# Rotary scores from two half-height parts, and the second rotary product ahead of the first head group

## The chip, the cores and the metric

The kernel runs on one NeuronCore of a Trainium2 chip. The metric is the device time of one execution in microseconds (us), of which lower is better. Engines are named as in the profile: PE (TensorE, with PEld for its weight loads), DVE (VectorE), ACT (ScalarE), POOL (GpSimd), SP (SyncE, which issues the weight transfers).

## The reference

Two decoder layers on 256 tokens of width 2048, each an attention mixer followed by a gated feed-forward block. Layer 1, which the change touches, is multi-head latent attention with 16 heads. From the normed input `h` it computes `cq = rms_norm(h @ wq_a)` (512 wide), from that the queries, 192 wide for each head: 128 plain columns `q_nope` and 64 rotary columns `q_rope`. From `h @ wkv_a` (576 wide) come the 512 latent columns `ckv` and ONE rotary key of 64 columns that all heads share. The scores of a head are

```
s = (q_nope . k_nope + q_rope . k_rope) * 192 ** -0.5     # causal, then softmax, then p @ v
```

All of it is in float32; the reference's rotary part is normed by head, multiplied by a gain and rotated with the position.

## The kernel before

Every large product is taken in "fp32r", a float32 form that TensorE runs in one pass, on a high part (the value rounded) and a low part (what the rounding left): high by high, high by low, low by high. Each weight piece of 128 x 512 is split by `Stream.split` (L92): ACT casts the high part (L104), DVE subtracts it (L105). Small products inside attention are plain float32 (F32), which TensorE runs as two instructions each.

The order of all work is written by hand. `quanta` is a list of PE products, one for each weight piece; `add` appends one and returns its index. `at(q, f)` hangs side work behind quantum q. The loop at L1049 goes through the quanta: it first splits pieces up to four ahead of q (L1052), then issues the product of q, then q's side work. Each engine executes its own instructions in the order in which that loop issues them, so DVE, ACT and POOL each have one queue, in which weight splitting and side work alternate. The weight units (4 pieces, 1 MB) are loaded on SP's queue three units ahead of the split (L96, L71); `units` (L138 to L155) must list them in the order of the quanta.

Layer 1's attention stage is planned from L818. Its quanta, in order:

- `wq_a` (16 quanta, `feat_major`), which leaves `cqT`.
- `rotary_queries(0, 2)` (L985): 4 quanta of `mla_wqr`, the rotary queries of heads 0 to 7. Its side work (`Heads` with 8 heads a tile, 64 wide): evacuation at its last quantum, squares, `rstd` on POOL, scaling, rotation, and 28 and 29 quanta after its last one the transposes `turned` (L442) and the copy `turned_out` (L454) into `qrT`.
- `wkv_a` (2 x 16 quanta, 288 columns each). Call the last of them q. Behind q hang `kva_stats` (L839, with a POOL power at L852), at q+3 `kva_scale` (L854), at q+3 and q+4 `kva_turn` (L878: transposes of `ckv`, evacuated into `ckvT`), at q+7 `kva_rotate` (L864), at q+9 `kr_turn` (L891: transposes of the rotary key).
- four head groups g of 4 heads: 4 quanta each of queries (`cqT`), keys and values (`ckvT`), in the order q, k, v for g = 0 and k, q, v after that. Behind group 0 stands `rotary_queries(1, 2)` (L1015), the rotary queries of heads 8 to 15. `plan_heads` (L622) hangs the norm and the transposes of each product behind it, `Head.plan` (L556) the head's scores (L474), softmax, transposes of the probabilities (`turn`, `turned`) and values.

For the rotary scores a tile of `qrT` holds two heads: the even head's 64 rotary rows on partitions 0 to 63, the odd head's on 64 to 127. `kr_turn` writes two key tiles of 128 rows, one with the key on the upper 64 rows and zeros below, one the other way round (POOL writes the zeros at L898, DVE copies at L899). The rotary product of a head (L489) is therefore a float32 product over 128 rows, of which 64 are multiplied by zeros. Per head there are two query blocks: 128 key columns for the first and 256 for the second.

Of the kernel before, what the change touches and what calls it, by code (L numbers as in the profile page):

```python
# [115 lines left out]
def trunk(ctx: ExitStack, tc: tile.TileContext, a, out):  # L116
# [28 lines left out]
    units += units_of("mla_wq_a")  # L145
    units += grouped("mla_wqr", 1, 0)
    units += units_of("mla_wkv_a", KVN)
    for g in range(4):
        if g == 1:
            units += grouped("mla_wqr", 1, 1)  # L150
        for name in ("mla_wkn", "mla_wqn", "mla_wv") if g else ("mla_wqn", "mla_wkn", "mla_wv"):
            units += grouped(name, 1, g)
    units += units_of("mla_wo")
# [199 lines left out]
    class Heads:  # L353
# [21 lines left out]

        def squares(self, t):
            for i in range(self.n):
                junk = att_pool.tile([P, P], F32, name="junk", bufs=2)
# [38 lines left out]
        def rotate(self, t, stages=(0, 1)):  # L417
            if not self.rot:
                return
            n, rot = self.n, self.rot  # L420
            hf = rot // 2
            tb, C, Sn = self.tabs
            ct = tb[:, C + t * rot : C + (t + 1) * rot]
            st = tb[:, Sn + t * rot : Sn + (t + 1) * rot]
            x = self.x[:, t]
            def over(s):
                return s[:, None, :].to_broadcast([P, n, s.shape[1]])

            def part(name):
                r = att_pool.tile([P, 16 * 32], F32, name=name, bufs=2)  # L430
# [38 lines left out]
    class Head:  # L469
# [4 lines left out]
        def scores(self):  # L474
            sc = ps_sc.tile([P, 512], F32, name="sc")
            qT, kT, i = self.qT(), self.kT(), self.i
            self.sc = sc
            if self.parts:

                (q0, q1), (k0, k) = qT, kT  # L480
                mm(sc[:, :P], q0[:, i], k0[:, i], start=True, stop=True)
                three(sc[:, P : 3 * P], q1[:, 0, i], q1[:, 1, i], k[:, 0, i], k[:, 1, i], True, True)
                return
            for q0, n, c in ((0, P, 0), (P, S, P)):
                o = sc[:, c : c + n]
                mm(o, qT[:, i, q0 : q0 + P], kT[:, i, :n], start=True, stop=self.rope is None)  # L486
                if self.rope is not None:
                    qr, kr = self.rope()
                    mm(o, qr[:, q0 : q0 + P], kr[:, :n], start=False, stop=True)  # L489

        def biased(self):
            self.s = att_pool.tile([P, 3 * P], F32, name="s", bufs=3)
# [30 lines left out]

        def turned(self):
            if not self.parts:
                self.pT = att_pool.tile([P, 3 * P], F32, name="pT", bufs=2)
# [294 lines left out]
    def open_mla():  # L821
        nonlocal att_pool
        ffn["stack"].close()
        att_pool = att2.enter_context(tc.tile_pool(name="att2", bufs=2))
        env["ckv"] = att_pool.tile([P, NT, 2 * KVN], F32, name="ckv", bufs=1)
        env["ckvT"] = att_pool.tile([P, 4, 2 * S], F32R, name="ckvT", bufs=1)
        env["cqT"] = att_pool.tile([P, 4, 2 * S], F32R, name="cqT", bufs=1)
        env["oT"] = att_pool.tile([P, H, 2 * S], F32R, name="oT", bufs=1)
        env["qrT"] = att_pool.tile([P, 8, S], F32, name="qrT", bufs=1)


    def kva_evac(state, half):
# [6 lines left out]
    def kva_stats():  # L839
        ss = small.tile([P, NT, 2], F32, name="kvss")  # L840
        for t in range(NT):
            for k, (lo, hi) in enumerate(((0, 512), (512, 576))):
                junk = att_pool.tile([P, 512], F32, name="kvjunk", tag="ro1", bufs=2)
# [18 lines left out]
            )  # L862

    def kva_rotate():  # L864
        env["krr"] = att_pool.tile([P, NT, 2, 64], F32, name="krr", bufs=1)
        for t in range(NT):
            x = env["ckv"][:, t, 512:]
            ct = tab[:, T_LC + t * 64 : T_LC + (t + 1) * 64]
            st = tab[:, T_LS + t * 64 : T_LS + (t + 1) * 64]
            t1 = att_pool.tile([P, 64], F32, name="kro1", bufs=2)  # L870
            t2 = att_pool.tile([P, 64], F32, name="kro2", bufs=2)
# [19 lines left out]
    def kr_turn():  # L891
        tp = ps_tp.tile([P, 512], F32, name="tp")
        for t in range(NT):
            nc.tensor.transpose(
                tp[:, t * P : (t + 1) * P], env["krr"][:, t].rearrange("p i d -> p (i d)"), ident
            )
        for i in range(2):
            nc.gpsimd.memset(env["kr"][i], 0.0)  # L898
            nc.vector.tensor_copy(env["kr"][i][i * 64 : (i + 1) * 64, :], tp[i * 64 : (i + 1) * 64, :S])  # L899


    cq = {}
# [54 lines left out]

    at(q_start + 20, gained_tables)

    def rotary_queries(u, step):  # L960
        state = {}
        for kt in range(4):
            q = add(tok_major, state, lambda: env["cqT"], kt, 3)
# [29 lines left out]
    def open_room():  # L993
        t = keep.tile([P, KD * 2 * S + 64], F32, name="room", tag="h")
        env["room"] = t[:, : 32 * S].rearrange("p (k s) -> p k s", k=32)
        env["kr"] = [env["room"][:, 28 + i] for i in range(2)]

    at(q, open_room)
    at(q, kva_stats)
    at(q + 3, kva_scale)  # L1000
    at(q + 7, kva_rotate)
    for r in range(4):
        at(q + 3 + r // 2, kva_turn, r)
    at(q + 9, kr_turn)

    def mla_tiles(g):
        i = 4 * (g % 2)
# [3 lines left out]
        env["v", g] = env["room"][:, 16 + i : 20 + i].rearrange("p (t c) s -> p t (c s)", t=NT)  # L1011

    for g in range(4):
        if g == 1:
            rotary_queries(1, 2)  # L1015
        for kind in "kqv" if g else "qkv":
            state = {}
            for kt in range(4):
# [10 lines left out]
        for i in range(4):  # L1029
            hd = Head(  # L1030
                4 * g + i, lambda g=g: env["qT", g], lambda g=g: env["kT", g], lambda g=g: env["v", g],
                i, lambda: env["oT"], MLA_SCALE,
                rope=lambda h=4 * g + i: (env["qrT"][:, h // 2, :], env["kr"][h % 2]),
            )
            q0 = q_q + 11 + 3 * i
            hd.plan(q0, q0 + 7)
# [131 lines left out]
```

## Time and profile before

| | us |
|---|---|
| median of 3 runs (2099.7 to 2100.92) | 2099.79 |
| the profiled execution | 2099.88 |
| its span in the trace | 2098.0 |
| PE busy | 2089.0 |
| PEld busy | 2014.2 |
| DVE busy | 1405.3 |
| ACT busy | 1138.3 |
| POOL busy | 45.6 |

The 1.88 us between the profiled execution and its span lie ahead of the first and behind the last instruction. Matmuls are pipelined, so the busy time of PE is no measure of what its products need; the distance between the starts of consecutive products is. Layer 1's attention stage runs from about 1133 us to about 1320 us of the span: the first product of `mla_wqr` starts at 1133.33, the last product of `wkv_a` at 1166.37, the first rotary score product (L489) at 1199.1, the last at 1306.9. In a row of the timeline the columns are start, duration, engine, line, operation, output and inputs, shapes, count, and in brackets the engine's idle time before it and what ended that.

### The profile page before, as it was taken

Reading aid. Unit: us, or ns where it says so; the run is one execution under the profiler, and the core shown is the slowest. Engines: PE = TensorE matmul, PEld = TensorE weight load, DVE = VectorE, ACT = ScalarE, POOL = GpSimd, SP = SyncE. Lnnn points to the kernel's source line nnn. Section 1 sums busy time; section 2 is a strip of 40 time slices with the busy share of each in tenths; the row PEclk is TensorE's granted clock in tenths of the full one; section 3 lists DMA queues with packets and bytes.
Section 4 is the critical chain, followed back from the end, with each engine's and each line's share of the span. In section 5 each row is a group of like instructions: output and inputs, shape, how many; then the busy total and the mean of one; then the engine's idle time right before and its main releaser. Section 6 shows DMA issues by size and latency. Waiting matters only on the chain.

```text
span 2098.0 us, 42200 instructions
## 1 busy us (share of the span) xinstructions
PE 2089.0 (100%) x16716; PEld 2014.2 (96%) x16716; DVE 1405.3 (67%) x3072; ACT 1138.3 (54%) x2238; POOL 45.6 (2%) x37
## 2 busy tenths in 40 slices
PE   9999999999999999999999999999999999999999
PEld 7888889999999999999999889999999999999999
DVE  6776776776666766655556786766766667655554
ACT  6555555655555555545555675655555555544443
POOL 0000000000000000000000110000000000000000
PEclk9999999999999999999999999999999999999999
DMA  7444445555555555555554533555555555555553
GB/s 272 161 170 173 170 171 185 194 188 198 195 190 200 191 191 201 194 190 198 194 191 159 175 139 108 195 181 201 187 196 199 187 199 195 189 205 209 193 207 131
DMA packets 59382, 391.83 MB, mean 187 GB/s; under 512 B 6960, under 2 KB 10032, under 8 KB 13232
## 3 DMA queue, kind: packets, MB, share of 16 engines
q1 hardware_dynamic: 59040, 388.87, 52.3%
q8 instruction: 131, 2.15, 0.4%
q14 instruction: 67, 0.55, 0.1%
q10 hardware_dynamic: 144, 0.26, 0.0%
HBM read 387.01 MB, written 2.10 MB: 185 GB/s over the span
## 4 chain that ended last, share of the span: by engine, by line
PE 96%; DVE 2%; POOL 0%; ACT 0%; issue 0%; DMA 0%; SPq 0%; ACTq 0%; DVEq 0%; POOLq 0%
PE acc L261 26%; PE acc L263 26%; PE acc L262 26%; PE acc L235 15%; PE tp L449 1%; DVE wlo L105 1%; PE sc L489 0%; PE sc L486 0%; PE tp L521 0%; POOL hr L392 0%; DVE junk L379 0%; PE sc L546 0%; DVE qk L405 0%; DMA xT<-in_xT 0%; PE sc L465 0%
## 5 line engine op out<-in xcount | busy, mean ns | idle before, releaser
L105 DVE TENSOR_TENSOR wlo<-raw,whi 128x512 fp32r<-128x512 f32 (+1 forms) x1480 | 1000.1, 684 | 399.0 <-ACT whi L104 396.0
L104 ACT CAST whi<-raw 128x512 fp32r<-128x512 f32 (+1 forms) x1479 | 871.6, 614 | 459.6 <-PE acc L262 212.3
L261 PE MATMUL acc<-h,whi 128*128 128x256 f32 x2880 | 796.1, 276 | 0.0
L263 PE MATMUL acc<-h,wlo 128*128 128x256 f32 x2880 | 795.9, 276 | 0.0
L262 PE MATMUL acc<-h,whi 128*128 128x256 f32 x2880 | 795.8, 276 | 0.0
L261 PEld LDWEIGHTS acc<-h,whi 128*128 128x128 f32 x2880 | 540.9, 188 | 0.0
L263 PEld LDWEIGHTS acc<-h,wlo 128*128 128x128 f32 x2880 | 540.9, 188 | 0.0
L262 PEld LDWEIGHTS acc<-h,whi 128*128 128x128 f32 x2880 | 540.9, 188 | 0.0
L262 PE MATMUL acc<-a,whi 128*128 128x256 f32 x1408 | 389.1, 276 | 0.0
L263 PE MATMUL acc<-a,wlo 128*128 128x256 f32 x1408 | 389.0, 276 | 0.0
L261 PE MATMUL acc<-a,whi 128*128 128x256 f32 x1408 | 389.0, 276 | 0.0
L235 PE MATMUL acc<-whi,h 128*128 128x512 f32 (+1 forms) x896 | 274.6, 381 | 0.0
L263 PEld LDWEIGHTS acc<-a,wlo 128*128 128x128 f32 x1408 | 264.4, 188 | 0.0
L262 PEld LDWEIGHTS acc<-a,whi 128*128 128x128 f32 x1408 | 264.4, 188 | 0.0
L261 PEld LDWEIGHTS acc<-a,whi 128*128 128x128 f32 x1408 | 264.4, 188 | 0.0
L235 PEld LDWEIGHTS acc<-whi,h 128*128 128x128 f32 x896 | 165.0, 188 | 30.0 <-ACT whi L104 0.7
L235 PE MATMUL acc<-wlo,h 128*128 128x512 f32 (+1 forms) x448 | 170.4, 381 | 2.1 <-DVE wlo L105 2.0
L261 PE MATMUL acc<-oT,whi 128*128 128x256 f32 x512 | 144.9, 283 | 0.0
L263 PE MATMUL acc<-oT,wlo 128*128 128x256 f32 x512 | 141.9, 277 | 0.0
L262 PE MATMUL acc<-oT,whi 128*128 128x256 f32 x512 | 141.7, 277 | 0.0
L740 DVE TENSOR_TENSOR g<-acc,rstd_b 128x256 f32<-128x256 f32 x88 | 37.5, 426 | 125.7 <-PE acc L263 122.7
L747 ACT ACTIVATE c<-g,par 128x256 f32<-128x256 f32 x88 | 53.1, 603 | 108.1 <-DVE g L740 108.1
(160 smaller groups left out, 1603.8 us busy)
## 6 DMA issues: line engine op xcount, KB each, us to landing
raw<-in_ffn_gu SPq DMA_DIRECT2D x176, 1024.0 KB, 4.8
raw<-in_ffn_down SPq DMA_DIRECT2D x88, 1024.0 KB, 4.8
raw<-in_moba_wk SPq DMA_DIRECT2D x16, 1024.0 KB, 4.9
raw<-in_moba_wv SPq DMA_DIRECT2D x16, 1024.0 KB, 4.8
raw<-in_moba_wo SPq DMA_DIRECT2D x16, 1024.0 KB, 4.8
raw<-in_mla_wo SPq DMA_DIRECT2D x16, 1024.0 KB, 4.8
raw<-in_moba_wq SPq DMA_DIRECT2D x13, 1024.0 KB, 4.9
raw<-in_mla_wkv_a SPq DMA_DIRECT2D x8, 576.0 KB, 3.7
```

The source lines that it names most:

```text
L104: self.nc.scalar.copy(hi[:, :n], w)
L105: self.nc.vector.tensor_tensor(lo[:, :n], w, hi[:, :n].bitcast(F32), op=ALU.subtract)
L235: mm(state["acc"][t][:, :n], src[:, kt, c : c + P], (t_lo if part == 1 else t_hi)[:, :n], start=kt == 0 and part == 0, stop=kt == k_last a ...
L261: mm(o, w_hi, src[:, kt, :S], start=first and k == 0, stop=False, skip_group_check=True)
L262: mm(o, w_hi, src[:, kt, S:], start=False, stop=False, skip_group_check=True)
L263: mm(o, w_lo, src[:, kt, :S], start=False, stop=kt == k_last, skip_group_check=True)
L449: nc.tensor.transpose(tp[:, (i * NT + t) * P : (i * NT + t + 1) * P], flat[:, t, c : c + P], ident)
L740: nc.vector.tensor_tensor(self.g[:, 2:], self.gate["acc"][:, :S], self.norm.rstd_b, op=ALU.mult)
L747: nc.scalar.activation(self.c, self.g[:, 2:], AF.Identity, bias=par[:, cb : cb + 1], scale=self.cw(2))
```

## The change

What it does:

- `qrT` becomes fp32r with one slot for each head (P x 16 x 256). A new function `rotary_out` takes the place of `turned_out` for the rotary queries: for each pair of transposed tiles ACT copies the upper and the lower 64 partitions (128 x 512 was one copy before, now there are two of 64 x 512), which gives the high part of each head on its own 64 rows; DVE subtracts to get the low part (two of 64 x 512), into a tile `qrlo` with two buffers; and two DMAs issued on POOL's queue move the low parts to the OTHER 64 partitions of the head's slot. Each head's stationary operand is then the high part on 64 rows and the low part on the other 64.
- `kr` becomes an fp32r tile with a high and a low part, both on all 128 rows (the transposed key is on both halves already): one ACT copy and one DVE subtraction in place of the two POOL memsets and two DVE copies.
- The rotary product of a head's block is two fp32r products (the key's high part, then its low part) in place of one float32 product.
- The second rotary product (`mla_wqr`, heads 8 to 15) moves from behind group 0 to directly behind `wkv_a`; its heads' work is hung 10 quanta later behind it (`later`), so that its transposes stand at q+42 and q+43 (before: q+44 and q+45). Group 0 moves 4 quanta back, the other groups keep their place. `kva_turn` moves to q+5 and q+6, `kr_turn` to q+10.
- For room: `junk`, `ro1`, `ro2`, `kro1`, `kro2` have one buffer in place of two, `krr` and the two `pT` tiles of layer 1 lie in the tile `room`.

```diff
@@ units
     units += units_of("mla_wkv_a", KVN)
+    units += grouped("mla_wqr", 1, 1)
     for g in range(4):
-        if g == 1:
-            units += grouped("mla_wqr", 1, 1)
...
@@ Head.scores
                     qr, kr = self.rope()
-                    mm(o, qr[:, q0 : q0 + P], kr[:, :n], start=False, stop=True)
+                    for part in range(2):
+                        mm(o, qr[:, q0 : q0 + P], kr[:, part, :n], start=False, stop=part == 1)
...
@@ open_mla
-        env["qrT"] = att_pool.tile([P, 8, S], F32, name="qrT", bufs=1)
+        env["qrT"] = att_pool.tile([P, H, S], F32R, name="qrT", bufs=1)
+        env["kr"] = att_pool.tile([P, 2, S], F32R, name="kr", bufs=1)
...
@@ kr_turn
-        for i in range(2):
-            nc.gpsimd.memset(env["kr"][i], 0.0)
-            nc.vector.tensor_copy(env["kr"][i][i * 64 : (i + 1) * 64, :], tp[i * 64 : (i + 1) * 64, :S])
+        hi, lo = env["kr"][:, 0], env["kr"][:, 1]
+        nc.scalar.copy(hi, tp[:, :S])
+        nc.vector.tensor_tensor(lo, tp[:, :S], hi.bitcast(F32), op=ALU.subtract)
...
+    def rotary_out(pair, j):
+        heads = env["qrT"].rearrange("p (j i) s -> p i j s", i=2)[:, :, j : j + 2]
+        tp = pair["tp"].rearrange("p (a s) -> p a s", a=2)
+        low = att_pool.tile([P, 2, S], F32R, name="qrlo", bufs=2)
+        halves = [slice(k * 64, (k + 1) * 64) for k in range(2)]
+        for i, rows in enumerate(halves):
+            nc.scalar.copy(heads[rows, i], tp[rows])
+        for i, rows in enumerate(halves):
+            nc.vector.tensor_tensor(low[rows], tp[rows], heads[rows, i].bitcast(F32), op=ALU.subtract)
+        for i, rows in enumerate(halves):
+            nc.gpsimd.dma_start(heads[halves[1 - i], i], low[rows])
+
-    def rotary_queries(u, step):
+    def rotary_queries(u, step, later=0):
...
         at(q, hs.evac)
+        q += later
...
-            at(q + step * 14 + i0 // 2, lambda p=pair, i0=i0: hs.turned_out(
-                env["qrT"][:, 4 * u : 4 * u + 4], p, i0))
+            at(q + step * 14 + i0 // 2, rotary_out, pair, 4 * u + i0)
...
     for r in range(4):
-        at(q + 3 + r // 2, kva_turn, r)
-    at(q + 9, kr_turn)
+        at(q + 5 + r // 2, kva_turn, r)
+    at(q + 10, kr_turn)
+    rotary_queries(1, 2, 10)
...
     for g in range(4):
-        if g == 1:
-            rotary_queries(1, 2)
```

More of the change, by code (lines that the diff above doesn't have):

```diff
@@ L377, in squares @@
             for i in range(self.n):
-                junk = att_pool.tile([P, P], F32, name="junk", bufs=2)
+                junk = att_pool.tile([P, P], F32, name="junk", bufs=1)
                 nc.vector.tensor_tensor_reduce(
@@ L429, in part @@
             def part(name):
-                r = att_pool.tile([P, 16 * 32], F32, name=name, bufs=2)
+                r = att_pool.tile([P, 16 * 32], F32, name=name, bufs=1)
                 return r[:, : n * rot].rearrange("p (n r) -> p n r", n=n)
@@ L525, in turned @@
             if not self.parts:
-                self.pT = att_pool.tile([P, 3 * P], F32, name="pT", bufs=2)
+                self.pT = env["pT"][self.h % 2]
                 nc.scalar.copy(self.pT, self.tp[:, : 3 * P])
@@ L842, in kva_stats @@
             for k, (lo, hi) in enumerate(((0, 512), (512, 576))):
-                junk = att_pool.tile([P, 512], F32, name="kvjunk", tag="ro1", bufs=2)
+                junk = att_pool.tile([P, 512], F32, name="kvjunk", tag="ro1", bufs=1)
                 nc.vector.tensor_tensor_reduce(
@@ L864, in kva_rotate @@
     def kva_rotate():
-        env["krr"] = att_pool.tile([P, NT, 2, 64], F32, name="krr", bufs=1)
         for t in range(NT):
@@ L869, in kva_rotate @@
             st = tab[:, T_LS + t * 64 : T_LS + (t + 1) * 64]
-            t1 = att_pool.tile([P, 64], F32, name="kro1", bufs=2)
-            t2 = att_pool.tile([P, 64], F32, name="kro2", bufs=2)
+            t1 = att_pool.tile([P, 64], F32, name="kro1", bufs=1)
+            t2 = att_pool.tile([P, 64], F32, name="kro2", bufs=1)
             nc.vector.tensor_tensor(t1, x, ct, op=ALU.mult)
@@ L995, in open_room @@
         env["room"] = t[:, : 32 * S].rearrange("p (k s) -> p k s", k=32)
-        env["kr"] = [env["room"][:, 28 + i] for i in range(2)]
+        env["krr"] = t[:, 31 * S : 32 * S].rearrange("p (t i d) -> p t i d", t=NT, i=2)
+        env["pT"] = [t[:, 28 * S + i * 3 * P : 28 * S + (i + 1) * 3 * P] for i in range(2)]
     at(q, open_room)
@@ L1032, in trunk @@
                 i, lambda: env["oT"], MLA_SCALE,
-                rope=lambda h=4 * g + i: (env["qrT"][:, h // 2, :], env["kr"][h % 2]),
+                rope=lambda h=4 * g + i: (env["qrT"][:, h], env["kr"]),
             )
```

## The prediction

> **What bounds the kernel now.** I read the page first: its totals, then the chain that ended last. The chain is PE for nearly the whole span, and the granted clock is full in every slice, so a change is worth what it takes off PE's queue or adds to PE's waiting.
>
> ```profile
> span 2098.0 us, 42200 instructions
> PEclk9999999999999999999999999999999999999999
> PE 96%; DVE 2%; POOL 0%; ACT 0%; issue 0%; DMA 0%; SPq 0%; ACTq 0%; DVEq 0%; POOLq 0%
> ```
>
> Next the windows of layer 1's attention (columns: length, then busy us of PE, PEld, DVE, ACT, POOL, then clock, DMA share, GB/s). PE lacks 2.1 us in the two windows behind `wkv_a`; everywhere else it is full, though DVE reaches 9.8 of 10 in one window.
>
> ```profile
> 1170.00:1180.00 10.00, 9.04 (x44) 7.12 (x43) 7.86 (x30) 6.10 (x13) 0.64 (x1) 1.00 0.43 147
> 1180.00:1190.00 10.00, 8.85 (x40) 6.40 (x39) 8.73 (x39) 5.11 (x10) 2.88 (x4) 1.00 0.48 169
> 1220.00:1230.00 10.00, 10.00 (x59) 8.48 (x58) 6.58 (x16) 9.11 (x26) 0.00 (x0) 1.00 0.29 106
> 1240.00:1250.00 10.00, 10.00 (x56) 8.49 (x55) 9.80 (x38) 7.17 (x20) 1.95 (x1) 1.00 0.41 156
> ```
>
> **Part 1: the score products.** PE's time per product is read from the starts in its timeline, not from the durations, which overlap. One head's two blocks:
>
> ```profile
> 1204.57 0.39 PE L489 MATMUL sc<-room,qrT 128*128 128x128 f32 x2
> 1204.79 0.60 PE L486 MATMUL sc<-room 128*128 128x256 f32 x2
> 1205.22 0.59 PE L489 MATMUL sc<-room,qrT 128*128 128x256 f32 x2
> ```
>
> The float32 rotary product over 128 columns takes 0.22 us (1204.57 to 1204.79), and one over 256 columns 0.43 (1204.79 to 1205.22, its equal L486): 0.65 per head, 16 heads. After the change each is two fp32r products. Their price over 256 columns is shown by layer 0's heads, over 512 by the big products, and the nearest rows for 128 columns are the transposes (128 columns, one weight load each) and a float32 product of ONE column (two instructions each, so two products make four):
>
> ```profile
> 84.54 0.28 PE L465 MATMUL sc<-k,q 128*128 128x256 f32 x1
> 84.66 0.28 PE L466 MATMUL sc<-k,q 128*128 128x256 f32 x1
> ...
> 1177.21 0.39 PE L235 MATMUL acc<-wlo,ckvT 128*128 128x512 f32 x1
> ...
> 1177.89 0.39 PE L235 MATMUL acc<-wlo,ckvT 128*128 128x512 f32 x1
> ...
> 1188.77 0.44 PE tp L449 x4
> ...
> 1136.07 0.50 PE L921 MATMUL tp<-ones,cacc 128*128 128x1 f32 x4
> 1136.43 0.49 PE L235 MATMUL acc<-whi,cqT 128*128 128x512 f32 x1
> ```
>
> Over 256 columns an fp32r product takes 0.12: two are 0.24 for 0.43, saving 0.19 per head. Over 512 it takes 0.227 (three in 0.68). For 128 columns no fp32r row exists. From below, 0.09: the one-column products take 0.36/4 each, so the weight load alone costs that. From above, 0.227, if so few columns were streamed four times each. I take 0.11, the transposes' 0.44/4, for they have the same columns and the same load: two are 0.22 for 0.22, no gain. So a head saves 0.19 and 16 save 3.0 us (bounds: 16 x 0.23 = 3.7 saved; with 0.227 the block costs 0.235 more, so 16 x 0.045 = 0.7 lost).
>
> The Trainium skill ("TensorE: Matmul & The Clock Gate", "Back-to-back issue gap") gives 55.6 ns for an isolated product of 128 columns; by that 16 heads would save 4.8 us. The same page ("LDWEIGHTS") puts a load of 128 columns at 107 ns, with which the one-column row's 0.09 nearly agrees.
>
> **Part 2: the stall behind `wkv_a`.** Here PE waits for DVE, in three places:
>
> ```profile
> 1170.37 0.39 PE L235 MATMUL acc<-whi,cqT 128*128 128x512 f32 x1
> 1171.52 0.30 PE L881 MATMUL tp<-ident,ckv 128*128 128x128 f32 x1 [0.76 <-DVE ckv L858]
> 1172.02 0.55 PE L881 MATMUL tp<-ident,ckv 128*128 128x128 f32 x3 [0.20 <-DVE ckv L858]
> ...
> 1180.83 0.39 PE L235 MATMUL acc<-whi,ckvT 128*128 128x512 f32 x1
> 1181.22 0.30 PE L894 MATMUL tp<-ident,krr 128*128 128x128 f32 x1
> 1181.86 0.33 PE L894 MATMUL tp<-ident,krr 128*128 128x128 f32 x1 [0.34 <-DVE krr L876]
> ...
> 1186.15 0.39 PE L235 MATMUL acc<-whi,cqT 128*128 128x512 f32 x1
> 1187.34 0.50 PE L235 MATMUL acc<-wlo,cqT 128*128 128x512 f32 x1 [0.81 <-DVE wlo L105]
> ```
>
> With 0.23 for a product of 512 columns and 0.11 for a transpose, the starts are late by 0.92 and 0.39 (transposes of `ckv`, for `kva_scale`), 0.16 and 0.53 (`krr`), and 0.96 (a low part): 3.0 us; the windows' 2.1 is less because modelled ends cover part. The change puts 4 quanta that need only `cqT` there and moves the transposes to q+5, two quanta or 2.7 us later, `kr_turn` one quantum. The third stall came because DVE, behind its copies for the key, waited for POOL's memsets, which stood behind a power:
>
> ```profile
> 1182.03 1.95 POOL L392 TENSOR_TENSOR hr<-hms,mhalf 128x8 f32<-128x8 f32 x1 [11.40 <-DVE hms L387]
> 1183.93 0.55 POOL L898 MEMSET room<- 128x256 f32 x2
> ...
> 1184.27 0.86 DVE L899 COPY room<-tp 64x256 f32<-64x256 f32 x2 [1.18 <-POOL room L898]
> ```
>
> The memsets go; the ACT copy and the DVE subtraction over 256 columns that replace the copies (less than the 0.5 and 0.63 us that 512 columns take below) wait for no POOL. I take all 3.0 us off (bounds 0 and 3.0).
>
> New work stands just ahead: `rotary_out` for heads 0 to 7, 28 and 29 quanta behind their product, so three ahead of the end of `wkv_a`.
>
> ```profile
> 1169.25 1.39 POOL L852 TENSOR_TENSOR kvr<-kvms,mhalf 128x4 f32<-128x4 f32 x1 [20.39 <-DVE kvms L850]
> ...
> 1163.10 0.59 ACT L457 COPY qrT<-tp 128x512 f32<-128x512 f32 x1 [1.58 <-PE tp L449]
> 1163.58 0.44 ACT L104 CAST whi<-raw 128x288 fp32r<-128x288 f32 x1
> 1164.33 0.59 ACT L457 COPY qrT<-tp 128x512 f32<-128x512 f32 x1 [0.31 <-PE tp L449]
> ...
> 1165.47 1.90 DVE L105 TENSOR_TENSOR wlo<-raw,whi 128x512 fp32r<-128x512 f32 x3 [0.96 <-ACT whi L104]
> ```
>
> A 64 x 512 copy or subtraction has the same columns as a 128 x 512 one, so I price each copy at ACT's step here (0.5 us) and each subtraction at DVE's (1.90/3 = 0.63). ACT gets two copies more (1.0 us), DVE four subtractions (2.5), and the low parts queue behind them. On ACT: copies to 1164.1, cast to 1164.5, copies to 1165.5. On DVE: the last two subtractions 1165.4 to 1166.65, then the low part of the first piece behind `wkv_a` to 1167.3. PE reaches that piece at 1166.5 and its second product at 1166.73: 0.6 us lost (0 to 1.5). Then `kva_stats` runs to 1170.3, the POOL power (1.39, first row above) to about 1171.9, `kva_scale` to 1173.3; PE comes to the transposes at 1173.9, so the old stall is gone by 0.6 us.
>
> **Part 3: the crowded stretch q+25 to q+41.** Group 0's heads move 4 quanta towards group 1's, while DVE's lead there is nearly used up already:
>
> ```profile
> 1241.88 0.28 DVE L495 CUSTOM_DVE_ANT_0 s<-sc,mask 128x128 f32<-128x128 f32 x1
> ...
> 1242.63 0.69 DVE L397 TENSOR_TENSOR qk<-qk,hr 128x512 f32<-128x512 f32 x1
> ...
> 1244.08 0.69 DVE L105 TENSOR_TENSOR wlo<-raw,whi 128x512 fp32r<-128x512 f32 x1
> ...
> 1250.35 0.16 DVE L511 RECIPROCAL sst<-sst 128x2 f32<-128x2 f32 x1
> ...
> 1251.01 0.69 DVE L105 TENSOR_TENSOR wlo<-raw,whi 128x512 fp32r<-128x512 f32 x1
> ```
>
> ```profile
> 1245.19 0.39 PE L235 MATMUL acc<-wlo,ckvT 128*128 128x512 f32 x1
> ```
>
> The low part of piece q+42 is ready at 1244.77 and first used at 1245.19: 0.4 us to spare. In these 17 quanta the shift brings one more `biased` (0.75 us, 1241.88 to 1242.63) and two more `normal` (0.66 each, 1250.35 to 1251.01) onto DVE, 2.1 us. Onto PE it brings three of group 0's score sets at 1.11 (twice 0.65, less 0.19) for two at 1.30, and one `turn` more (three transposes, 0.33), while group 1's three sets get cheaper by 0.57: 0.73 + 0.33 - 0.57 = 0.5. DVE falls behind by 1.6, 1.2 more than it can. Behind it, at q+42 and q+43, four subtractions (2.5 us) fall where the first loss has given DVE its lead back and PE has more to do (the two transposes of rotary queries, 0.9, stand there too); I put 0.3 on them. I take 1.5 lost (bounds 0 and 1.2 + 2.5 = 3.7).
>
> The rest costs nothing on PE: single buffers for `junk`, `ro`, `kro` are written and read by DVE alone, in order; SP's list only swaps two 1 MB loads; the eight moves are 1 MB in a stretch where the DMA share is 0.3 to 0.5 of 16 engines. A move of 128 KB has this row (columns: size each, us to landing):
>
> ```profile
> out<-xT SPq DMA_DIRECT2D x16, 128.0 KB, 1.9
> ```
>
> The second set leaves at q+42 and is read at q+47, about 10 us on, against ACT 1.0, DVE 1.3 with a lag of 2, POOL's issue and 1.9 landing: 3 us to spare at 1.1 us of issue.
>
> **Sum.** -3.0 (scores) -3.0 (old stalls) +0.6 +1.5 = -3.9 on the profiled execution's 2099.88, so 2096.0; the median (2099.79) is 0.1 lower, which changes nothing.
>
> **Rivals.**
> - *128 columns of fp32r are dear* (0.227): scores then lose 0.7 instead of saving 3.0: 2099.7. For it: no row shows such a product. Against: the float32 one of 128 columns needs just 0.11 per instruction. 0.10.
> - *They are cheap*, by the slope from 512 to 256 columns (0.107): 0.12 - 0.05 = 0.06 each: 0.10 more per head saved, 1.6 in all: 2094.4. Against: the one-column row. 0.10.
> - *DVE and ACT become the bound in q+25 to q+47*: the four subtractions, 2.5 us, fall on PE in full, 2.2 more than the 0.3: 2098.2. For it: 9.80 of 10 busy. Against: 6.58 in 1220 to 1230 leaves room. 0.10.
> - *POOL's queue, slower than before*: the first four moves stand ahead of the POOL power for `kva_scale`, and DVE's low parts stand behind that scale. They can start at 1164.3; the power must start by 1170.8 to be in time, so 1.6 us per issue is free. Beyond it PE loses 4 x (d - 1.6) - 0.6: at d = 2.8 the gain is gone, from 3.8 the kernel is slower by over 0.2%. No row shows an issue on POOL; its rows above run from 0.28 (one of the two memsets) to 1.95 (a power), and I take 1.1, their middle. At 4.5 the time would be 2107. The Trainium skill ("SBUF — State Buffer", "SBUF: two separate sides") says that DVE's two-port modes lock POOL out of writing descriptors, 3.1 us instead of 0.62 in its example; by that it is about 2101.4 here, and no trace of before can show it. 0.13, of which 0.11 slower.
>
> **How the numbers follow.** My case has 0.57, from 2093.9 to 2098.0 as the lost 0.6 and 1.5 vary; nearly half of it below 2095.6, which is 0.2% under before, about what a measurement can tell from no change. Faster: 0.29 + 0.10 = 0.39. Same: 0.28 + 0.10 + 0.10 + 0.02 = 0.50. Slower: 0.11. The range runs from 2093.2 (3.7 saved on scores, no loss beyond 0) to 2100.0 (dear columns), leaving out POOL's case.
>
> **What would show it.** L489 of fp32r: two products over 256 columns 0.24 apart from the next, over 128 columns 0.22. PE full from 1170 to 1190, with a short wait for `wlo` near 1166.7 and one near q+42. POOL's issues short, and `kva_scale` not waiting for `kvr`. Wrong it would be if 128 columns took 0.45, if PE waited for `tp` of `ckv` still, or if waits for `wlo` summed to over 4 us between 1200 and 1260.

## The result and the profile after

The changed kernel takes 2105.88 us (median of 8 runs, 2105.43 to 2106.80), the kernel before in the same job 2099.78 (8 runs, 2099.61 to 2100.92): the ratio is 1.0028, with the interval 1.0019 to 1.0037. It is slower by 6.1 us where 3.9 us of gain was forecast, and it lies outside the range of the prediction.

The page of the changed kernel, its span and its chain of waits: PE's share of the chain has fallen from 96% to 91%, and DVE's has gone from 2% to 6%.

```profile
span 2104.5 us, 42227 instructions
PE 91%; DVE 6%; ACT 1%; issue 1%; POOL 1%; DMA 0%; SPq 0%; ACTq 0%; POOLq 0%; DVEq 0%
```

So DVE has become late somewhere. Where is told by milestones: the first and last start of a group of products. First those of the kernel before (line, form, count, then min/median/max ns, and the first and last start). L261 with `h` is the first product of layer 0's feed-forward block, L261 with `a` the last product of the program, L235 with `cqT` the first product of `mla_wqr`, with which the changed part of layer 1 begins.

```profile
L261 PE MATMUL acc<-h,whi x2880: 275/276/367, 392.1 to 1854.5; 128*128 128x256 f32 x192
L261 PE MATMUL acc<-a,whi x1408: 275/276/277, 871.7 to 2093.9; 128*128 128x256 f32 x176
L235 PE MATMUL acc<-whi,cqT x96: 388/394/580, 1133.3 to 1261.2; 128*128 128x512 f32 x96
```

The same three of the changed kernel (its lines stand one lower):

```profile
L260 PE MATMUL acc<-h,whi x2880: 276/276/367, 398.7 to 1860.8; 128*128 128x256 f32 x192
L260 PE MATMUL acc<-a,whi x1408: 276/276/276, 878.3 to 2100.2; 128*128 128x256 f32 x176
L234 PE MATMUL acc<-whi,cqT x96: 388/393/486, 1139.9 to 1268.9; 128*128 128x512 f32 x96
```

The loss is 6.6 us at 392.1, and still 6.6 where layer 1's changed part begins (1133.3 to 1139.9). From there to the last product it takes 960.6 us before and 960.3 after. So two things have to be explained: all of the loss lies in layer 0, where no order and no score was changed, and in layer 1, where all the work was done, nothing was gained.

The same product of both kernels, found by counting, tells how the 6.6 us come about. The one that starts at 13.35 us before starts at 14.00 after, 0.65 later, and the first square of a norm starts only at 53.1 and 53.7. Such a difference in the first microseconds comes and goes between executions: among the kernels below that have two buffers for `junk` the feed-forward block starts anywhere from 391.5 to 394.3 us. The rest of the delay, 5.9 us, comes in eight steps of about 0.7 between 60 and 300 us. (For layer 1 its own length is therefore the surer measure beside the medians; it is given below where it matters.)

PE's waits between 40 and 340 us, layer 0's attention, before:

```profile
PE acc L235 <- DVE wlo L105: 1.5, 3, 0.8
```

and after (total us, times, longest):

```profile
PE acc L234 <- DVE wlo L105: 6.5, 9, 1.1
```

PE waits nine times in place of three for the low part of a weight piece, 5.0 us more in all. DVE has nothing new to do there, but one thing takes longer. Before, DVE's timeline at two neighbouring squares of a norm, with the read of the first one's sum between them:

```profile
181.39 0.28 DVE L379 CUSTOM_DVE_ANT_0 junk<-qk 128x128 f32<-128x128 f32 x1
181.60 0.08 DVE L379 DVE_READ_ACCUMULATOR2_ANT ss<- 128x1 f32 x1
181.60 0.29 DVE L379 CUSTOM_DVE_ANT_0 junk<-qk 128x128 f32<-128x128 f32 x1
```

After:

```profile
184.98 0.29 DVE L378 CUSTOM_DVE_ANT_0 junk<-qk 128x128 f32<-128x128 f32 x1
185.20 0.08 DVE L378 DVE_READ_ACCUMULATOR2_ANT ss<- 128x1 f32 x1
185.31 0.29 DVE L378 CUSTOM_DVE_ANT_0 junk<-qk 128x128 f32<-128x128 f32 x1
```

The instruction itself lasts as long as before (0.29). Its neighbour now starts 0.33 us after it, not 0.21: before, two squares overlapped by 0.08; now the second starts only when the first has ended. `junk` is the tile that each square writes and that nobody reads; the change gave it one buffer. The second write to it therefore waits for the first one to be over, on DVE's own queue. The profile doesn't call that a wait: in the waits it appears as PE waiting for `wlo`, which stands behind the squares.

The 64-wide squares of the rotary queries in layer 1 show the same. Before they are 0.14 us apart, after 0.26:

```profile
1197.71 0.22 DVE L379 CUSTOM_DVE_ANT_0 junk<-qr 128x64 f32<-128x64 f32 x1
1197.85 0.22 DVE L379 CUSTOM_DVE_ANT_0 junk<-qr 128x64 f32<-128x64 f32 x1
```

```profile
1148.31 0.22 DVE L378 CUSTOM_DVE_ANT_0 junk<-qr 128x64 f32<-128x64 f32 x1
1148.57 0.23 DVE L378 CUSTOM_DVE_ANT_0 junk<-qr 128x64 f32<-128x64 f32 x1
```

The addition is 0.12 us for either width. A set of four heads has three such gaps, one of eight heads seven: layer 0's 64 squares in sets of four have 48 gaps, 5.8 us of DVE, which is six gaps or 0.7 us for each of the eight steps; layer 1's 64 of four and 32 of eight have 48 + 28 = 76, 9.1 us.

**Theory A**: the single buffer of `junk` costs 0.12 us per gap on DVE, and PE loses what DVE has no slack to give. **Rival B**: the other single buffers (`ro1`, `ro2`, `kro1`, `kro2`), or the places that tiles got when the pool shrank, slow DVE, and the pitch of the squares is a sign only. **Rival C**: the loss belongs to the new scores and order, and layer 0 is displaced by something else.

### The profile page after: what moved, and what is told of

It is laid out like the page before. It is cut to its first block, busy times and chain, and to the rows that moved or that the text cites. A ratio compares the mean times of both kernels' runs of the same rounds, so it can differ in the third digit from the quotient of the medians.

```text
span 2104.5 us, 42227 instructions
## 1 busy us (share of the span) xinstructions
PE 2087.2 (99%) x16716; PEld 2011.7 (96%) x16716; DVE 1419.6 (67%) x3079; ACT 1141.9 (54%) x2243; POOL 50.6 (2%) x43
## 4 chain that ended last, share of the span: by engine, by line
PE 91%; DVE 6%; ACT 1%; issue 1%; POOL 1%; DMA 0%; SPq 0%; ACTq 0%; POOLq 0%; DVEq 0%
PE acc L260 26%; PE acc L262 26%; PE acc L261 26%; PE acc L234 10%; DVE wlo L105 2%; DVE junk L378 1%; POOL hr L391 1%; DVE qk L404 1%; PE tp L448 1%; PE tp L522 0%; PE sc L485 0%; ACT qk L373 0%; ACT whi L104 0%; DMA xT<-in_xT 0%; PE sc L547 0%
## 5 line engine op out<-in xcount | busy, mean ns | idle before, releaser
L105 DVE TENSOR_TENSOR wlo<-raw,whi 128x512 fp32r<-128x512 f32 (+1 forms) x1480 | 999.6, 684 | 391.5 <-ACT whi L104 388.8
L261 PE MATMUL acc<-h,whi 128*128 128x256 f32 x2880 | 794.9, 276 | 0.0
L261 PEld LDWEIGHTS acc<-h,whi 128*128 128x128 f32 x2880 | 540.6, 188 | 0.0
L261 PE MATMUL acc<-a,whi 128*128 128x256 f32 x1408 | 388.6, 276 | 0.0
L261 PEld LDWEIGHTS acc<-a,whi 128*128 128x128 f32 x1408 | 264.3, 188 | 0.0
L261 PE MATMUL acc<-oT,whi 128*128 128x256 f32 x512 | 141.6, 277 | 0.0
L234 PEld LDWEIGHTS acc<-wlo,h 128*128 128x128 f32 x448 | 84.2, 188 | 28.7 <-DVE wlo L105 15.5
```

The source lines that it names most:

```text
L105: self.nc.vector.tensor_tensor(lo[:, :n], w, hi[:, :n].bitcast(F32), op=ALU.subtract)
L234: mm(state["acc"][t][:, :n], src[:, kt, c : c + P], (t_lo if part == 1 else t_hi)[:, :n], start=kt == 0 and part == 0, stop=kt == k_last a ...
L261: mm(o, w_hi, src[:, kt, S:], start=False, stop=False, skip_group_check=True)
```

## The experiments

All times are medians, ratios are to the kernel before in the same job (2099.94 to 2100.12 there).

**One buffer for `junk`, in the kernel before.** The cleanest cut: nothing else of the change is in it.

```diff
-                junk = att_pool.tile([P, P], F32, name="junk", bufs=2)
+                junk = att_pool.tile([P, P], F32, name="junk", bufs=1)
```

> The kernel before with one buffer for the squares' scratch tile junk, nothing else. Theory A (a square that writes the tile of the square just ahead of it waits for that one to have ended, 0.12 us each): squares 0.33 us apart in place of 0.215, layer 0 6.6 us longer, layer 1 another 1.5 to 3, so 2107.5 to 2109.5. Theory B (layer 0 got slower because all of its tiles lie at other addresses, junk's wait is nothing): 2099.8 to 2101.

Measured: 2110.76 us, ratio 1.0052 (1.0039 to 1.0064), 10.7 us slower. The pitch is that of the changed kernel:

```profile
185.91 0.29 DVE L379 CUSTOM_DVE_ANT_0 junk<-qk 128x128 f32<-128x128 f32 x1
186.24 0.29 DVE L379 CUSTOM_DVE_ANT_0 junk<-qk 128x128 f32<-128x128 f32 x1
```

and PE's waits between 40 and 340 us are those of the changed kernel, to the tenth:

```profile
PE acc L235 <- DVE wlo L105: 6.5, 9, 1.1
```

One number of one line makes the whole loss of layer 0, without the scores and without the order. C falls for layer 0. The loss is 1.3 us above A's upper end: in layer 1, with the old order, PE's waits for `wlo` grow from 0.8 to 3.9 us and for `krr` from 0.3 to 1.1.

**One buffer for the rotation's tiles, in the kernel before.**

```diff
-                r = att_pool.tile([P, 16 * 32], F32, name=name, bufs=2)
+                r = att_pool.tile([P, 16 * 32], F32, name=name, bufs=1)
```

and likewise `kvjunk`, `kro1` and `kro2`.

> The kernel before with one buffer for ro1, ro2, kro1 and kro2 and for the scratch of kva_stats, and two for junk. Theory A: only the four reductions of kva_stats and the two rounds of kva_rotate follow each other directly, so DVE loses some 0.6 us in layer 1, on the path at most: 2099.5 to 2100.7. Theory B (addresses): layer 0 slower by some us as in the kernel after: 2103 to 2106.

Measured: 2100.79, ratio 1.0003 (0.9994 to 1.0012). The median is 0.1 us above A's range and 2.2 below B's; layer 1's own length is 961.0 us against 960.6. These tiles cost nothing that stands clear of the interval, and the first half of B falls. Its second half, the places of the tiles, is settled by the experiment with bfloat16 below.

**Two buffers for `junk`, in the changed kernel.** `kro1` and `kro2` move into the buffers of `ro1` and `ro2`, to make room.

```diff
-                junk = att_pool.tile([P, P], F32, name="junk", bufs=1)
+                junk = att_pool.tile([P, P], F32, name="junk", bufs=2)
@@
-            t1 = att_pool.tile([P, 64], F32, name="kro1", bufs=1)
-            t2 = att_pool.tile([P, 64], F32, name="kro2", bufs=1)
+            t1 = att_pool.tile([P, 512], F32, name="kro1", tag="ro1", bufs=1)[:, :64]
+            t2 = att_pool.tile([P, 512], F32, name="kro2", tag="ro2", bufs=1)[:, :64]
```

> The kernel after with two buffers for junk again (kro1 and kro2 share the tiles ro1 and ro2, for room). Theory A: layer 0 back to its old length (-6.6), in layer 1 squares 0.12 us closer, 2 to 3 us less lost there: 2096 to 2098. Theory B: no change by junk, 2104 to 2106.

Measured: 2096.27, ratio 0.9982 (0.9973 to 0.9991). This is the kernel that the prediction described, 0.3 us from its 2096.0. PE's waits in layer 0's attention are back at those of before:

```profile
PE acc L234 <- DVE wlo L105: 1.5, 3, 0.8
```

**Two buffers in layer 0 alone**, in the changed kernel; `ckv` is there in layer 1 only.

```diff
-                junk = att_pool.tile([P, P], F32, name="junk", bufs=1)
+                junk = att_pool.tile([P, P], F32, name="junk", bufs=1 if "ckv" in env else 2)
```

> The kernel after with two buffers for junk in layer 0 only, one in layer 1. Theory A: 6.6 us less than after, so 2099.3; the distance to the kernel with two everywhere (2 to 3 us) is what single junk costs in layer 1. Theory B: 2104 to 2106.

Measured: 2100.22, ratio 1.0 (0.9991 to 1.0009). This is 0.9 above the 2099.3 of the expectation, and the distance to two buffers everywhere is twice what was expected. The 6.6 us from which the expectation reckoned held the 0.65 us of the first microseconds. So the single buffer costs 2105.88 - 2100.22 = 5.7 us in layer 0, where DVE's own delay is 48 x 0.12 = 5.8, and 2100.22 - 2096.27 = 4.0 in layer 1, of DVE's 9.1. That is how 960.3 against 960.6 came about: the 4 us that layer 1 gained it lost again to its own squares.

**One buffer of double width, alternate halves**, in the kernel before: consecutive squares write different bytes of one tile. Is it the bytes, or the tile?

```diff
-                junk = att_pool.tile([P, P], F32, name="junk", bufs=2)
+                both = att_pool.tile([P, 2 * P], F32, name="junk", bufs=1)
+                junk = both[:, i % 2 * P : (i % 2 + 1) * P]
```

> The kernel before with ONE buffer of twice the width for junk, of which successive squares write the left and the right half in turn. If the wait goes by the bytes that two squares share, it is gone: squares 0.215 us apart, 2099.5 to 2100.7. If it goes by the buffer as a whole: 0.33 us apart, 2110 to 2111.5 as with one buffer of single width.

Measured: 2110.04, ratio 1.0047 (1.0034 to 1.0061): as slow as one buffer. The squares start 0.32 us apart:

```profile
186.09 0.28 DVE L380 CUSTOM_DVE_ANT_0 junk<-qk 128x128 f32<-128x128 f32 x1
186.41 0.29 DVE L380 CUSTOM_DVE_ANT_0 junk<-qk 128x128 f32<-128x128 f32 x1
```

The wait goes with the buffer as a whole. No byte is written twice in a row here, and the second square still waits for the first: what two buffers buy is that the wait is put on the square two back, which is over by then (it started 0.42 us earlier and lasts 0.29). In this edit each square asks the pool for the buffer anew; whether two halves of a tile that is taken once would wait was not tried.

**The new order alone**, in the kernel before: units, `kva_turn`, `kr_turn` and `rotary_queries(1, 2, 10)` as in the change, scores, `turned_out` and buffers as before.

```diff
+    units += grouped("mla_wqr", 1, 1)
     for g in range(4):
-        if g == 1:
-            units += grouped("mla_wqr", 1, 1)
@@
-        at(q + 3 + r // 2, kva_turn, r)
-    at(q + 9, kr_turn)
+        at(q + 5 + r // 2, kva_turn, r)
+    at(q + 10, kr_turn)
+    rotary_queries(1, 2, 10)
```

> The kernel before (float32 rotary scores, zeros, one copy for the transposed queries) with the new order alone. If the order is worth the stalls: 2097 to 2098.3, for here no new low part stands ahead of the moved product either. If it is worth nothing: 2099.8 to 2100.5. The difference to the kernel after with two buffers is then what the score parts are worth net of their own DVE work: 16 x 0.19 = 3.0 less about 1.2.

Measured: 2096.36, ratio 0.9982 (0.9973 to 0.9991): 3.7 us gained, 0.6 better than the expectation's lower end. By layer 1's own length it is 3.5 (957.1 against 960.6). PE has no wait left from 1120 to 1330 us, and the two windows behind `wkv_a`, in which PE lacked 2.1 us, are full:

```profile
1170.00:1180.00 10.00, 10.00 (x50) 8.29 (x49) 8.94 (x27) 6.67 (x14) 1.90 (x3) 1.00 0.62 229
1180.00:1190.00 10.00, 10.00 (x47) 8.25 (x46) 8.97 (x43) 6.80 (x12) 1.95 (x1) 1.00 0.40 131
```

**The new scores with the old order**, in the changed kernel with two buffers: the diff above taken back.

> The kernel after with two buffers for junk, and the order of before: second rotary product behind group 0, ckv's transposes at q+3 and q+4, the rotary key's at q+9. If the order is worth the 3.0 us of stalls that the prediction reads behind wkv_a (and brings 0.3 to 1.5 of loss elsewhere), this is 1.5 to 3 slower than with the new order: 2097.8 to 2099.3. If the score products alone bring all of the 3.8 us, the order is worth nothing: 2096 to 2096.7.

Measured: 2100.16, ratio 1.0 (0.9991 to 1.0008). A miss: 0.9 us above the upper end, and no gain at all from the new scores with the old order. PE's timeline behind `wkv_a` (in brackets the idle time before):

```profile
1168.47 0.50 PE L235 MATMUL acc<-wlo,cqT 128*128 128x512 f32 x1 [1.00 <-DVE wlo L105]
...
1172.23 0.39 PE L235 MATMUL acc<-whi,cqT 128*128 128x512 f32 x1
1174.16 0.30 PE L883 MATMUL tp<-ident,ckv 128*128 128x128 f32 x1 [1.54 <-DVE ckv L861]
1174.66 0.55 PE L883 MATMUL tp<-ident,ckv 128*128 128x128 f32 x3 [0.20 <-DVE ckv L861]
```

`rotary_out`'s subtractions make the old stall at `ckv` grow from 0.76 to 1.54. And shortly behind that idle stretch, at about 1175.5, the granted clock (the third number from the end) is halved for some 3.4 us, until about 1178.9:

```profile
1175.00:1175.50 0.50, 0.50 (x4) 0.42 (x3) 0.00 (x0) 0.48 (x2) 0.00 (x0) 0.96 1.00 426
1175.50:1176.00 0.50, 0.50 (x3) 0.38 (x2) 0.47 (x2) 0.50 (x2) 0.00 (x0) 0.50 1.12 475
```

Over the 10 us from 1170 the mean is 0.83, that is 1.7 us of PE lost. The account of layer 1 against before: -3.0 (scores), +0.5 (waits for `wlo` 1.3, before 0.8), +0.7 (`ckv` 1.7, before 1.0), -0.1 (`krr` 0.2, before 0.3), +0.3 (a wait for `qrlo` to free its bank) and +1.7 (clock): +0.1, and the layer took 0.2 us longer (960.8). So with the old order the 3.0 of the new scores are eaten by the waits and the clock. With the new order they fare little better at first: the order alone takes 2096.36, order and scores together 2096.27 (957.1 and 956.3 in layer 1), for the work that the scores put on ACT and DVE makes PE lose most of the 3.0 again (the part on why the prediction was wrong has the terms).

The drop of the clock stands in this profile; over the span the mean clock was 0.999 in seven of this kernel's 11 executions (median 2100.46) and 1.0 in the other four (2099.29), and 1.0 in every execution of the two kernels with the new order just named. A mean of 0.999 also stands on one execution of the kernel before (2102.35) and one of the kernel with bfloat16 below (2097.69), of which there is no trace. That the idling caused the drop was not tried by itself. The Trainium skill ("TensorE: Matmul & The Clock Gate", "What's actually happening") says that the clock is halved after an idle window of about 3.4 us and comes back after about as much work. The 3.4 us at half clock agree. The idle time was not that long here, 1.54 and 0.20 us preceded the drop; if it was the cause, less than the Trainium skill's window was enough.

**The copies and subtractions of the first set 4 quanta earlier** (24 and 25 quanta behind the product, not 28 and 29), in the changed kernel with two buffers:

```diff
-    rotary_queries(0, 2)
+    rotary_queries(0, 2, 0, 12)
```

where the fourth argument replaces the 14 of `q + step * 14 + i0 // 2`.

> The kernel after with two buffers for junk, and the first set of rotary queries split 24 and 25 quanta behind its product in place of 28 and 29, so four quanta of wkv_a earlier. If the 1.0 and 0.26 us that PE waits at the end of wkv_a come from those four subtractions standing ahead of the low parts, they go: 2095 to 2095.6, against 2096.3. If that wait has another cause: 2096 to 2096.7.

Measured: 2096.22, ratio 0.998 (0.9971 to 0.9989): a miss, the same as without it. The wait has moved with its cause: 0.26 and 0.87 us, on two pieces of `wkv_a` at 1162.89 and 1164.82.

**The same with the two pairs apart**, at 24 and 28 quanta:

```diff
-    rotary_queries(0, 2)
+    rotary_queries(0, 2, 0, (24, 28))
```

> The kernel after with two buffers for junk, and the first set's two pairs split 24 and 28 quanta behind their product in place of 28 and 29. If the wait at the end of wkv_a (1.0 and 0.26 us) comes from two pairs following each other within one quantum of 0.79 us, each with 1.2 us of ACT and 1.4 of DVE ahead of the low parts, it goes or halves: 2094.8 to 2095.7 against 2096.3. If one pair alone is too much: 2096 to 2096.7.

Measured: 2096.41, ratio 0.9981 (0.9972 to 0.999). A miss again: each pair alone makes PE wait.

```profile
1163.54 0.40 PE L234 MATMUL acc<-wlo,h 128*128 128x288 f32 x1 [0.69 <-DVE wlo L105]
...
1168.11 0.40 PE L234 MATMUL acc<-wlo,h 128*128 128x288 f32 x1 [0.70 <-DVE wlo L105]
```

So it is not only the amount of work at one place. ACT's and DVE's rows for these two pairs tell what else it may be:

```profile
1160.37 1.18 ACT L969 CAST qrT<-tp 64x512 fp32r<-64x512 f32 x2 [2.29 <-PE tp L448]
...
1164.94 1.18 ACT L969 CAST qrT<-tp 64x512 fp32r<-64x512 f32 x2 [1.94 <-PE tp L448]
```

```profile
1161.58 1.41 DVE L971 TENSOR_TENSOR qrlo<-tp,qrT 64x512 fp32r<-64x512 f32 x2 [1.11 <-ACT qrT L969]
1163.02 1.57 DVE L105 TENSOR_TENSOR wlo<-raw,whi 128x288 fp32r<-128x288 f32 x4
```

ACT stands idle for 2.29 us with the copy at the head of its queue, since PE has not come to the transposes; DVE stands idle for 1.11 behind ACT. In that time no piece is split, and when the copies and subtractions have run, PE has used up the pieces that were ready. The theory is that the low part at 1163.02 is late by the round trip from PE through ACT and DVE, more than by their load. The experiment with the two quanta below tests it.

**Two buffers for `junk` in the room of one**: since nothing reads it, it can be bfloat16. Otherwise the changed kernel as it is.

```diff
-                junk = att_pool.tile([P, P], F32, name="junk", bufs=1)
+                junk = att_pool.tile([P, P], BF16, name="junk", bufs=2)
```

> The kernel after with two buffers for junk in bfloat16 (the tile is never read), so with no more memory than one in float32. Theory A (the wait of a square for the one before it in the same buffer): as with two float32 buffers, 2096 to 2097. If the second buffer's gain came from kro1 and kro2 sharing tiles there, or from other addresses: 2104 to 2106.

Measured: 2095.90, ratio 0.998 (0.9971 to 0.9989). It beats both kernels, by 4.2 us and by 10, with one line edited. `junk` takes no more room here than in the changed kernel and nothing else is moved, so the second half of B falls too: it is the second buffer, not the places of the other tiles. Its lead over the kernel with two float32 buffers, the order alone and the two placements (2096.2 to 2096.4) is within the intervals.

**The copies and subtractions two quanta behind their transposes**, in the kernel with the bfloat16 tile: two more pieces are split ahead of them, and by then the transposes should be done. First with the transposes where they were (28 and 29 quanta behind the product), then with the pairs apart (24 and 28).

```diff
-            at(q + step * 14 + i0 // 2, lambda p=pair, i0=i0: hs.turned(None, p, i0))
-            at(q + step * 14 + i0 // 2, rotary_out, pair, 4 * u + i0)
+            at(q + outs[i0 // 2], lambda p=pair, i0=i0: hs.turned(None, p, i0))
+            at(q + outs[i0 // 2] + lag, rotary_out, pair, 4 * u + i0)
...
-    rotary_queries(0, 2)
+    rotary_queries(0, 2, 0, (28, 29), 2)
```

> The kernel with the bfloat16 scratch tile (2095.9), with the copies and subtractions of the first set (rotary_out of heads 0 to 7) two quanta behind their transposes, at 30 and 31 quanta behind the product. If the wait at the end of wkv_a (about 1.6 us) comes from ACT and DVE standing idle at the head of their queues until the transposes are done (ACT idle 2.3 us ahead of the copies), two pieces more are split ahead of them and PE waits for less: 1 us or more gained, 2094.4 to 2095.2. If it comes from the work itself (1.18 us on ACT, 2.8 on DVE) or from the limited number of split buffers, nothing changes: 2095.6 to 2096.3.

Measured: 2095.13, ratio 0.9975 (0.9965 to 0.9985): inside the range, but 0.8 us gained is short of the 1 that was expected, and by layer 1's own length it is 0.4 (955.8 against 956.2). Both waits at the end of `wkv_a` have gone. In their place PE waits for 1.0 us some five microseconds later, for a low part that now stands behind `kva_stats` on DVE:

```profile
1172.11 0.50 PE L234 MATMUL acc<-wlo,cqT 128*128 128x512 f32 x1 [0.98 <-DVE wlo L105]
```

With the order alone, where DVE has no such subtractions, PE waits nowhere here. So with both pairs close together their work still costs PE a wait; it only falls later.

> The same, with the transposes of the two pairs at 24 and 28 quanta and their copies and subtractions at 26 and 30. By the idle heads of the queues both waits of 0.7 us go, and the 0.4 us before them stays: 2094.2 to 2095.0. By the work or the buffers they stay: 2095.6 to 2096.5.

Measured: 2094.29, ratio 0.9973 (0.9963 to 0.9983), the best of all: 5.6 us under the kernel before (2099.94 there). Both waits of 0.7 are gone. Layer 1 takes 954.8 us, 1.4 less than with the bfloat16 tile alone. (Five of the nine executions took 2093.7 to 2094.3 and four 2095.0 to 2095.9; the profiled one is of the latter, and its feed-forward block of layer 0 starts 0.9 us later than that of the bfloat16 kernel, 393.1 against 392.2.) PE's waits from 1120 to 1330 us are now

```profile
PE tp L448 <- DVE qr L439: 0.4, 1, 0.4
PE tp L448 <- DVE qrlo L971: 0.3, 1, 0.3
```

and ACT is idle for 0.61 us ahead of the first pair's copies (2.29 without the lag) and not at all ahead of the second's (1.94).

The same work with the transposes at the same two places, and two pieces more ahead of it in the queues, costs no wait for a low part. That bears out the round trip for pairs that stand apart. It needs both: apart without the lag gained nothing (2096.41 against 2096.27, with two float32 buffers), the lag without apart 0.8 us (2095.13 against 2095.90), both together 1.6 (2094.29). That the copies merely stand at better places, at 26 and 30 quanta, is a rival that was not tried; against it speaks that ACT's idle time ahead of them went as the theory has it.

## Why the prediction was wrong

**The step that failed** is one clause: "single buffers for `junk`, `ro`, `kro` are written and read by DVE alone, in order". It took being on one engine for being free. For `ro` and `kro` that held (0.7 us by the median, within the interval). For `junk` it cost 9.6 us of PE (2105.88 to 2096.27): 5.7 in layer 0, 4.0 in layer 1. The trace of before had the row that spoke against it: two squares start 0.21 us apart and last 0.28, so they overlap, and an overlap is what one buffer takes away. 0.07 x 124 gaps would already have been 8.7 us on DVE, in stages where PE already waited for `wlo`. None of the rivals had this mechanism either; that is why the range missed.

With that term out, the rest can be judged in the changed kernel with two buffers, against before: predicted -3.9, measured -3.8 by medians and -4.3 by layer 1's length (956.3 against 960.6). That the two are so near is partly luck, as the terms show.

**Scores, -3.0: right.** One head's two blocks start at 1244.67 and the next product at 1245.78, 1.11 us. Before, where the first product behind a head starts early in the records, the one to compare is the second behind it: 1198.90 to 1200.44 before, 1.54, and 1244.67 to 1246.02 here, 1.35. That is the forecast 0.19 less, and all 16 heads have it. The changed kernel:

```profile
1244.67 0.38 PE L485 MATMUL sc<-room 128*128 128x128 f32 x2
...
1245.36 0.59 PE L490 MATMUL sc<-kr,qrT 128*128 128x256 f32 x2
1245.78 0.40 PE L234 MATMUL acc<-whi,ckvT 128*128 128x512 f32 x1
```

With 0.65 for the plain products and 0.24 for two of 256 columns, 0.22 is left for two of 128: neither dear nor cheap. The 55.6 ns for an isolated product, which the prediction took from the Trainium skill ("TensorE: Matmul & The Clock Gate", "Back-to-back issue gap"), are not reached: here each product has a weight load of its own, which that section says the isolated figure leaves out. Both rivals on the columns fall.

**Old stalls, -3.0: right, a little small.** In the changed kernel with two buffers the first transposes of `ckv` come with no wait; the order alone gained 3.5 in layer 1. Of the further 0.5, 0.4 stand in the trace of before right behind the third stall: three distances of 0.34, 0.44 and 0.34 from 1187.34 to 1189.74, where 0.23 is the usual one.

```profile
1183.42 0.60 PE L882 MATMUL tp<-ident,ckv 128*128 128x128 f32 x4
```

**Low part late at the end of `wkv_a`, +0.6: right in kind, too small.** In the kernel with two buffers, DVE and PE there:

```profile
1165.61 1.41 DVE L971 TENSOR_TENSOR qrlo<-tp,qrT 64x512 fp32r<-64x512 f32 x2 [2.30 <-PE tp L448]
1167.06 0.46 DVE L105 TENSOR_TENSOR wlo<-raw,whi 128x288 fp32r<-128x288 f32 x1
1167.55 1.41 DVE L971 TENSOR_TENSOR qrlo<-tp,qrT 64x512 fp32r<-64x512 f32 x2
1168.99 1.89 DVE L105 TENSOR_TENSOR wlo<-raw,whi 128x512 fp32r<-128x512 f32 x3
```

```profile
1168.34 0.39 PE L234 MATMUL acc<-whi,cqT 128*128 128x512 f32 x1
1169.73 0.50 PE L234 MATMUL acc<-wlo,cqT 128*128 128x512 f32 x1 [1.01 <-DVE wlo L105]
```

Two subtractions take 1.41, not 1.26, and the pair's second stands behind a low part. The product at 1169.73 was due at 1168.57, 1.16 late, and one piece earlier PE lost another 0.4: 1.6 us. The prediction counted the work of ACT and DVE but not the time that they stand idle for PE's transposes with it (the 2.30 in the first row). In the last experiment, where that time is short and the pairs stand apart, no wait for a low part is left.

**Crowded stretch, +1.5: too large.** Between 1180 and 1330 us PE has one wait, for a bank that the subtraction frees:

```profile
1248.07 0.63 PE L448 MATMUL tp<-ident,qr 128*128 128x128 f32 x4 [0.32 <-DVE qrlo L971]
```

By the distance of starts it is 0.5 (1247.35 to 1248.07, due after 0.23). The 0.3 that the prediction put on the four subtractions at this place was about right; the 1.2 that it put on the shift of group 0 is not there at all, and with the order alone PE has no wait in this stretch. The two sizing errors are of opposite sign: +1.6 and +0.5 where +0.6 and +1.5 stood, so the sum was kept by luck. -3.0 - 3.5 + 1.6 + 0.5 = -4.4 beside the measured -4.3. Set against the order alone, the new scores bring 3.0 and lose 2.1 of it again, and 0.8 is what layer 1 shows (956.3 against 957.1); only with the lag and the pairs apart is it 2.3 (954.8). The rival in which DVE and ACT become the bound in q+25 to q+47 falls too.

**POOL's queue: refuted.** The changed kernel's issues, on POOL:

```profile
1173.56 1.34 POOL L973 DMA_DIRECT2D qrT<-qrlo  x2 [16.46 <-DVE qrlo L971]
1175.48 1.30 POOL L973 DMA_DIRECT2D qrT<-qrlo  x2 [0.57 <-DVE qrlo L971]
1180.12 1.41 POOL L854 TENSOR_TENSOR kvr<-kvms,mhalf 128x4 f32<-128x4 f32 x1 [3.34 <-DVE kvms L852]
```

Some 0.65 us each, below the 1.1 that was taken and the 1.6 that was free; POOL then stood idle for 3.34 us until DVE had done its part for the power of `kva_scale`. The lock of which the Trainium skill tells ("SBUF — State Buffer", "SBUF: two separate sides"), 3.1 us in its example, does not show. That example has DVE run a `tensor_copy`; beside the issues here DVE ran subtractions, so whether a copy would lock POOL out no run here shows.

## What to carry to other kernels

A scratch tile that nobody reads is still an output. If instructions of one engine follow each other closely, look whether their rows overlap (start plus duration against the next start): the overlap is what a single buffer takes away, times the number of neighbours, and it appears under another name, as a late product of the same engine. Before dropping a buffer for room, look for a smaller type: bfloat16 gave two buffers in the room of one and 10 us back. And where side work runs through three engines, hang the later steps behind more of the main work, so that no queue stands idle with them at its head, and keep the pieces of that work apart: both together gave 1.6 us here, where moving all of it together gave none.

## What the runs showed of the hardware

- A DVE instruction that had to wait for the one right before it started 0.12 us later than one that had not: 0.33 after its neighbour, not 0.21, at 128 columns, 0.26 and not 0.14 at 64. The wait is for the buffer, not for the bytes (alternate halves of one buffer that each square takes anew: 0.32).
- The two moves of a pair occupied POOL for 1.30 to 1.34 us together, and landed 3.4 us after the issue in the median, against 1.9 for the results of 128 KB that SP writes out in the kernel before (loads of 128 KB into SBUF at its start: 3.7).
- About 1.7 us of idle PE preceded a stretch of 3.4 us at half the granted clock (the new scores with the old order; whether it caused it is open); with one buffer for `junk`, in the kernel before, waits of up to 1.2 us preceded none, the clock being 1.0 in all five executions.
